# Making the modulation tiles of the last two sub-layers earlier, in steps of half a tile

## The chip, the cores and the metric

The kernel runs on one core of one Trainium2 chip. The metric is the device time of one launch in microseconds (us). A core has TensorE (PE) for matrix products, VectorE (DVE), ScalarE (ACT), GpSimd (POOL) and SyncE (SP). SP issues most loads here.

## The reference

One inference step of a two-layer encoder, for a prompt of 512 frames and a sample of 64 frames (576 columns in all, 1024 channels, float32). Each layer has three sub-layers: a feed-forward, a token mixer and a feed-forward. The mixer of the first layer is a gated delta rule beside a short convolution, that of the second is stick-breaking attention with 16 heads. What matters for this change is the modulation, which each sub-layer takes from a conditioning vector `c` of the prompt and of the sample:

```python
cond = jax.nn.silu(c)
for l in range(DEPTH):
    mod = (cond @ ada_w[l] + ada_b[l]).reshape(b, N_SUB, 3, D_MODEL)
    shift, scale, gate = mod[:, :, 0], mod[:, :, 1], mod[:, :, 2]
    hh = _modulated_norm(x, norm_g[l, 0], shift[:, 0], scale[:, 0])
    x = x + 0.5 * gate[:, 0, None] * _swiglu(hh, ff_w_in[l, 0], ff_w_out[l, 0])
    ...
```

`ada_w[l]` is 1024 x 9216, so that each layer has nine vectors `j` of 1024 channels: shift, scale and gate of sub-layer 0 (`j` 0 to 2), of the mixer (3 to 5) and of the second feed-forward (6 to 8).

## The kernel before, in words

**The order of the work.** The program runs feed-forward (0, 0), mixer 0, feed-forwards (0, 2) and (1, 0), mixer 1 and feed-forward (1, 2). The text calls the feed-forwards the first to the fourth, the fourth also the last. All products are split: a weight and an activation are each written as a high and a low part (`wh`, `wl`; `XH`, `XL`), and three matmuls stand for one. Weights come by SP's DMA into a ring of three `stage` buffers (`w_dma`), ACT copies the high part, and DVE (sometimes POOL with a DMA) makes the low part.

**A feed-forward** (`ffn`, L843) has three chunks of 8, 8 and 6 column tiles of the hidden layer. For each tile it makes gate and up products from `XH` and `XL`, and `HH`, `HL` from them; after each chunk comes an output projection, whose evacuation (`residual`, L752) multiplies by the gate and adds to `x`. The first tiles of the first chunk are plain; the others go through `dense7` (L529), which makes a pair of products in seven block products instead of eight. Its operands are sums of activations (`TH`, `TL`) and of weights (`ss`), made on DVE, and DVE and ACT put the seven results together (`sg`, `up`, `hm`). Behind the last output projection of a sub-layer, the norm for the next one starts (`last_pairs`, L809; `start_sub`, L832).

**Mixer 1** (`mixer1`, L1503) makes q, k and v for eight pairs of heads, and runs one attention task (`att_pair`) for each pair behind the other. For each of nine query blocks, PE makes scores, ACT two sigmoids (`sg`, `sn`), DVE a scan (`cp`) and a product, PE transposes, ACT and DVE copy the result (`wt`), and PE multiplies by v. The tasks run between the dense matmuls of q, k, v, and of the first part of the output projection.

**The planner.** The instructions of each engine run in the order in which the program is written, and that order is made by a scheduler in the kernel (`Sched`, L257) over an account of the engines' times (`Model`). After each group of three dense matmuls, `tick` (L284) lets each task that is due take a step. A task yields the time at which it is next due, on PE's account (`S.clock`); `until` (L296) runs tasks until something has been made. `M.t["DVE"]` is the account of DVE.

**The modulation.** The vectors are made on DVE: a tile of 128 channels of one `j` is a load of 128 x 1024 float32 from `in_ada` into `aw` (`ada_dma`, L762), and for prompt and sample (`g`) one `scalar_tensor_tensor` that multiplies it by the broadcast `cond` (`cb`) and sums along the row into `mod`; the products themselves go to `jk` and are not used (`ada_tile`, L768). The text calls one such instruction a step. `ada_end` adds the bias after eight tiles. `ada_task` (L792) does this for a list of (l, j), a tile per interval `every` (in ns of the account), and only when the account has DVE no more than 1000 ns ahead. With two `aw` buffers (`bufs=2`) the next tile's load is issued just before this tile's steps. With one (`bufs=1`), load and steps of the same tile are apart by part of the interval. `hold` keeps the task back from a sub-layer's last output projections until the next sub-layer's second half has been normed.

Where it is made before: the shifts and scales of feed-forward 0 at the start, (0, 2) to (0, 7) in feed-forward (0, 0) with 6.2 us (L1793), (0, 8) and (1, 0) to (1, 4) in (0, 2) and (1, 0) with 9.5 us (L1802), (1, 5) to (1, 7) in mixer 1 with one buffer and 8.5 us (L1809), and (1, 8) in feed-forward (1, 2) with 8 us (L1814). The norms wait for their shift and scale (`out.need`), `residual` for the gate, and `mixer1` waits for its task before the last part of the output projection (L1668).

Of the kernel before, what the change touches and what calls it, by code (L numbers as in the profile page):

```python
# [107 lines left out]
def outs(nk):  # L108

    n = 2 if nk > 4 else (4 if nk > 2 else 8)  # L110
    return [tuple(range(m, m + n)) for m in range(0, 8, n)]
# [192 lines left out]
def encoder_step(ctx: ExitStack, tc: tile.TileContext, a, o):  # L304
    nc = tc.nc
    M = Model()
# [12 lines left out]
    S = Sched(M, lambda: psum.free("a"))  # L319
# [22 lines left out]
    cb = base.tile([P, 2, D], F32, name="cb")  # L342
# [403 lines left out]
    def split(src, ks):  # L746
        for t0, t1 in HALF:
            for i in ks:
                A.activation(XH[:, i, t0:t1], src[:, i, t0:t1], AF.Copy)
                V.tensor_sub(XL[:, i, t0:t1], src[:, i, t0:t1], XH[:, i, t0:t1].bitcast(F32))  # L750
# [9 lines left out]
    aw = {}  # L760

    def ada_dma(pool, todo, bufs):  # L762
        if todo:
            l, n = todo.pop(0)
            aw[l, n] = pool.tile([P, D], F32, name="aw", bufs=bufs)
            dma(aw[l, n], a["ada"][l, n])

    def ada_tile(pool, cb, l, j, kt):  # L768
        w = aw.pop((l, j * 8 + kt))
        for g in range(2):  # L770
            jk = pool.tile([P, D], mybir.dt.float8e4, name="jk")
            V.scalar_tensor_tensor(jk, w, 1.0, cb[:, g, :], op0=OP.mult, op1=OP.mult,
                                   accum_out=mod[:, l, j, kt, g:g + 1], saturate=False)
# [3 lines left out]
    def ada_end(l, j, k0=0, n=8):  # L777
        if k0 + n == 8:
            made.add((l, j))
        m = mod[:, l, j, k0:k0 + n]  # L780
        b = sm["ada_b"][:, l, j * 8 + k0:j * 8 + k0 + n].unsqueeze(2).to_broadcast([P, n, 2])
        V.tensor_add(m, m, b)
        s, kind = divmod(j, 3)
        if kind == 1:
            gn = sm["norm_g"][:, l * 3 + s, k0:k0 + n].unsqueeze(2).to_broadcast([P, n, 2])
            V.scalar_tensor_tensor(m, m, 1.0, gn, op0=OP.add, op1=OP.mult)
        if kind == 2 and s != 1:
            V.tensor_scalar(m, m, 0.5, None, op0=OP.mult)
# [3 lines left out]
    def ada_task(pool, todo, every, bufs=2):  # L792
        ahead = [(l, j * 8 + kt) for l, j in todo for kt in range(8)]
        for _ in range(bufs - 1):
            ada_dma(pool, ahead, bufs)
        yield S.clock + every
        for l, j in todo:
            for kt in range(8):
                while hold[0]:
                    yield S.clock + 1000.0  # L800
                ada_dma(pool, ahead, bufs)
                if bufs == 1:
                    yield S.clock + every - 3000.0
                ada_tile(pool, cb, l, j, kt)
                yield max(S.clock + (3000.0 if bufs == 1 else every), M.t["DVE"] - 1000.0)
            ada_end(l, j)


# [691 lines left out]
        return last_pairs(npool, 0, 1, ABO[1], modulated(npool, 0, 2))  # L1500


    def mixer1(pool, task, npool, at):  # L1503
        so = pool.tile([P, 8, NT], F32, name="so")
        qbH = pool.tile([P, 9, P], F32R, name="qbH")
        qbL = pool.tile([P, 9, P], F32R, name="qbL")
# [154 lines left out]
        for gi, ks in enumerate(SBO):  # L1661
            S.finish(att_tasks[ks[-1]])
            split(so, ks)
            if gi < len(SBO) - 1:
                for ms in outs(len(ks)):
                    dense(lambda g, half, ps: residual(1, 1, ms[g], half, ps), ks=ks, inter=ms[0] == 0)
            else:
                S.finish(at)  # L1668
                return last_pairs(npool, 1, 1, ks, modulated(npool, 1, 2))


    npool = Ring(M, ctx.enter_context(tc.tile_pool(name="npool", bufs=1)), 1)
# [14 lines left out]
    task = {}  # L1687

    with tc.tile_pool(name="ada", bufs=1) as ap, tc.tile_pool(name="ffn", bufs=1) as fp:
        ap, fp = Ring(M, ap), Ring(M, fp)  # L1690
# [40 lines left out]
        for m in range(8):  # L1731
            for half in range(2):
                stats(npool, m, half, V)
            if m % 2:
                g, h = m // 4, m // 2 % 2
# [55 lines left out]
        feed.scales = scales, scales_out, scales_end  # L1791
        task = feed
        at = S.spawn(ada_task(ap, [(0, j) for j in range(2, 8)], 6200.0))  # L1793
        S2M[0] = True
        task = ffn(0, 0, fp, task, modulated(npool, 0, 1))
        assert at[2]
    with tc.tile_pool(name="m0", bufs=1) as mp:
        mp = Ring(M, mp)
        task = mixer0(mp, task, npool)
    with tc.tile_pool(name="ada", bufs=1) as ap, tc.tile_pool(name="ffn", bufs=1) as fp:  # L1800
        ap, fp = Ring(M, ap), Ring(M, fp)
        at = S.spawn(ada_task(ap, [(0, 8)] + [(1, j) for j in range(5)], 9500.0))  # L1802
        task = ffn(0, 2, fp, task, modulated(npool, 1, 0))
        task = ffn(1, 0, fp, task, modulated(npool, 1, 1))
        assert at[2]
    S2M[0] = False
    with tc.tile_pool(name="m1", bufs=1) as mp:
        mp = Ring(M, mp)
        at = S.spawn(ada_task(mp, [(1, j) for j in (5, 6, 7)], 8500.0, 1))  # L1809
        task = mixer1(mp, task, npool, at)  # L1810
    with tc.tile_pool(name="ffn", bufs=1) as fp:
        fp = Ring(M, fp)
        yo["pool"] = fp
        at = S.spawn(ada_task(fp, [(1, 8)], 8000.0))  # L1814
        task = ffn(1, 2, fp, task, final)
        S.finish(task[0])
        S.finish(task[1])
# [96 lines left out]
```

## Time and profile before

| | |
|---|---|
| time, median of 3 runs | 2474.02 us (2473.24 to 2474.09) |
| the profiled execution | 2477.48 us |
| its span, first to last instruction | 2475.6 us |
| mean granted TensorE clock | 0.969 |
| PE busy, weight loads busy | 2358.8 us, 2278.5 us |
| DVE, ACT, POOL busy | 1784.2, 1091.2, 339.6 us |
| HBM read, written | 261.44 MB, 11.51 MB |

The profile is one execution. Times count from its first instruction. "Busy" of PE is modelled, since matmuls are pipelined: the records of one engine overlap, and a busy time is the length of their union. "Idle before" an instruction, and what ended it, are worked out from the semaphores. In a row, `jk<-aw,cb` means an instruction that writes `jk` from `aw` and `cb`. The helper that issues most instructions is line 191, so nearly all rows have L191, and are told apart by their tiles.

### The profile page before, as it was taken

The page shows a single profiled execution, that of the slowest core. Times are in us where ns is not written, and L with a number is a line of the kernel's source. Part 1 is how long each engine was busy: PE and PEld are TensorE (multiplying, and loading weights), DVE is VectorE, ACT ScalarE, POOL GpSimd, SP SyncE. Part 2 cuts the span into 40 slices and gives each one's busy share as a digit, 9 for nine tenths or more (in the row PEclk, how much of TensorE's full clock was granted, in tenths as well). Part 3 has the DMA queues.
Part 4 walks back from the last instruction along what each step waited for, and adds up shares of the span by engine and source line. Part 5 has one row for each costly group of instructions (what it writes and reads, how often), then busy time and mean ns, then how long its engine had stood idle before and what let it go on. Part 6 is the DMA issues. An engine that isn't in the chain of part 4 may idle for free. (4 is left out here: it accounts for less than half of the span.)

```text
span 2475.6 us, 45399 instructions
## 1 busy us (share of the span) xinstructions
PE 2358.8 (95%) x18364; PEld 2278.5 (92%) x18364; DVE 1784.2 (72%) x3456; ACT 1091.2 (44%) x1984; POOL 339.6 (14%) x467
## 2 busy tenths in 40 slices
PE   7989899999999999999999999999999999999998
PEld 5989899988878899999999999999888879999998
DVE  7688978588687578697967756466567777848474
ACT  4334526443322255263534446255555555425252
POOL 4100000342222240000022000003000004000001
PEclk9999999998889899999999999999999999999999
DMA  6656655232122246465636445352544325322222
GB/s 238 181 170 189 199 180 152 92 103 59 47 67 79 74 125 182 150 207 166 177 119 171 144 111 137 93 130 83 174 138 148 119 81 145 126 87 86 94 90 77
DMA packets 107349, 320.98 MB, mean 130 GB/s; under 512 B 26194, under 2 KB 28498, under 8 KB 106884
## 3 DMA queue, kind: packets, MB, share of 16 engines
q1 hardware_dynamic: 95188, 272.99, 33.0%
q0 software_dynamic: 11952, 45.09, 9.9%
q8 instruction: 145, 2.38, 0.4%
q14 instruction: 64, 0.52, 0.1%
HBM read 261.44 MB, written 11.51 MB: 110 GB/s over the span
## 5 line engine op out<-in xcount | busy, mean ns | idle before, releaser
L191 PE MATMUL d<-XH,wh 128*128 128x288 f32 x2304 | 714.8, 310 | 14.3 <-ACT XH L191 6.1
L191 PE MATMUL d<-XL,wh 128*128 128x288 f32 x2304 | 697.0, 303 | 11.3 <-POOL XL L191 8.0
L191 PE MATMUL d<-XH,wl 128*128 128x288 f32 x2304 | 695.3, 302 | 3.3 <-DMA wl<-stage 1.7
L191 PEld LDWEIGHTS d<-XH,wh 128*128 128x128 f32 x2304 | 447.3, 194 | 27.4 <-ACT XH L191 11.3
L191 PEld LDWEIGHTS d<-XL,wh 128*128 128x128 f32 x2304 | 447.5, 194 | 17.1 <-POOL XL L191 12.4
L191 PEld LDWEIGHTS d<-XH,wl 128*128 128x128 f32 x2304 | 447.2, 194 | 4.9 <-DVE wl L191 2.7
L191 PE MATMUL d<-HH,wh 128*128 128x288 f32 x1408 | 417.9, 297 | 3.9 <-ACT HH L191 3.9
L191 PE MATMUL d<-HL,wh 128*128 128x288 f32 x1408 | 418.3, 297 | 3.5 <-DVE HL L191 3.5
L191 ACT ACTIVATE wh<-stage 128x1024 fp32r<-128x1024 f32 (+3 forms) x345 | 319.9, 939 | 227.9 <-PE d L191 222.5
L191 PE MATMUL d<-HH,wl 128*128 128x288 f32 x1408 | 415.7, 295 | 0.0
L191 DVE TENSOR_TENSOR wl<-stage,wh 128x1024 fp32r<-128x1024 f32 (+3 forms) x259 | 268.7, 1043 | 113.0 <-ACT wh L191 110.6
L191 DVE SCALAR_TENSOR_TENSOR jk<-aw,cb 128x1024 fp8e4<-128x1024 f32 x256 | 315.4, 1232 | 36.0 <-DMA aw<-in_ada 31.4
L191 PE MATMUL d<-TH,wh 128*128 128x288 f32 x1056 | 312.1, 296 | 12.8 <-ACT sg L191 12.7
L191 PE MATMUL d<-TL,wh 128*128 128x288 f32 x1056 | 312.2, 296 | 0.0
L191 PE MATMUL d<-TH,wl 128*128 128x288 f32 x1056 | 311.9, 295 | 0.2
L191 DVE SCALAR_TENSOR_TENSOR x<-d,mod,x 128x64 f32<-128x64 f32 (+2 forms) x384 | 146.6, 412 | 218.3 <-PE d L191 216.8
L191 PEld LDWEIGHTS d<-HL,wh 128*128 128x128 f32 x1408 | 265.7, 189 | 6.2 <-DVE HL L191 6.2
L191 PEld LDWEIGHTS d<-HH,wh 128*128 128x128 f32 x1408 | 265.5, 189 | 4.7 <-ACT HH L191 4.4
L191 PEld LDWEIGHTS d<-HH,wl 128*128 128x128 f32 x1408 | 265.9, 189 | 0.0
L191 PEld LDWEIGHTS d<-TH,wh 128*128 128x128 f32 x1056 | 198.6, 188 | 16.4 <-ACT sg L191 16.3
L191 PEld LDWEIGHTS d<-TH,wl 128*128 128x128 f32 x1056 | 198.8, 188 | 0.8 <-DVE wl L191 0.6
L191 PEld LDWEIGHTS d<-TL,wh 128*128 128x128 f32 x1056 | 198.3, 188 | 0.0
(328 smaller groups left out, 3440.8 us busy)
## 6 DMA issues: line engine op xcount, KB each, us to landing
stage<-in_w SPq DMA_DIRECT2D x301, 512.0 KB
aw<-in_ada SPq DMA_DIRECT2D x128, 512.0 KB
wl<-stage POOLq DMA_DIRECT2D x59, 512.0 KB, 4.6
stage<-in_w SPq DMA_DIRECT2D x36, 384.0 KB
TL<-XL POOLq DMA_DIRECT2D x8, 576.0 KB, 8.6
TL<-ss POOLq DMA_DIRECT2D x8, 576.0 KB, 5.8
TL<-in_ada SPq DMA_DIRECT2D x8, 512.0 KB
stage<-in_w SPq DMA_DIRECT2D x8, 320.0 KB
```

The source lines that it names most:

```text
L191: r = real(*args, **kw)
```

## The change

The task now goes through a tile in two steps, each followed by its own wait; the branch for one buffer goes. The two feed-forwards between the mixers get all of (0, 8) and (1, 0) to (1, 8) with an interval of 8.0 us; mixer 1 and the last feed-forward have no task any more, and mixer 1 doesn't wait for one. The task of the first feed-forward keeps its list and its 6.2 us, but runs through the same loop.

```diff
--- before.py
+++ after.py
@@ -765,9 +765,9 @@
             aw[l, n] = pool.tile([P, D], F32, name="aw", bufs=bufs)
             dma(aw[l, n], a["ada"][l, n])
 
-    def ada_tile(pool, cb, l, j, kt):
-        w = aw.pop((l, j * 8 + kt))
-        for g in range(2):
+    def ada_tile(pool, cb, l, j, kt, gs=(0, 1)):
+        w = aw[l, j * 8 + kt]
+        for g in gs:
             jk = pool.tile([P, D], mybir.dt.float8e4, name="jk")
             V.scalar_tensor_tensor(jk, w, 1.0, cb[:, g, :], op0=OP.mult, op1=OP.mult,
                                    accum_out=mod[:, l, j, kt, g:g + 1], saturate=False)
@@ -799,10 +799,9 @@
                 while hold[0]:
                     yield S.clock + 1000.0
                 ada_dma(pool, ahead, bufs)
-                if bufs == 1:
-                    yield S.clock + every - 3000.0
-                ada_tile(pool, cb, l, j, kt)
-                yield max(S.clock + (3000.0 if bufs == 1 else every), M.t["DVE"] - 1000.0)
+                for g in range(2):
+                    ada_tile(pool, cb, l, j, kt, (g,))
+                    yield max(S.clock + every / 2, M.t["DVE"] - 1000.0)
             ada_end(l, j)
 
 
@@ -1500,7 +1499,7 @@
         return last_pairs(npool, 0, 1, ABO[1], modulated(npool, 0, 2))
 
 
-    def mixer1(pool, task, npool, at):
+    def mixer1(pool, task, npool):
         so = pool.tile([P, 8, NT], F32, name="so")
         qbH = pool.tile([P, 9, P], F32R, name="qbH")
         qbL = pool.tile([P, 9, P], F32R, name="qbL")
@@ -1665,7 +1664,6 @@
                 for ms in outs(len(ks)):
                     dense(lambda g, half, ps: residual(1, 1, ms[g], half, ps), ks=ks, inter=ms[0] == 0)
             else:
-                S.finish(at)
                 return last_pairs(npool, 1, 1, ks, modulated(npool, 1, 2))
 
 
@@ -1799,19 +1797,17 @@
         task = mixer0(mp, task, npool)
     with tc.tile_pool(name="ada", bufs=1) as ap, tc.tile_pool(name="ffn", bufs=1) as fp:
         ap, fp = Ring(M, ap), Ring(M, fp)
-        at = S.spawn(ada_task(ap, [(0, 8)] + [(1, j) for j in range(5)], 9500.0))
+        at = S.spawn(ada_task(ap, [(0, 8)] + [(1, j) for j in range(9)], 8000.0))
         task = ffn(0, 2, fp, task, modulated(npool, 1, 0))
         task = ffn(1, 0, fp, task, modulated(npool, 1, 1))
         assert at[2]
     S2M[0] = False
     with tc.tile_pool(name="m1", bufs=1) as mp:
         mp = Ring(M, mp)
-        at = S.spawn(ada_task(mp, [(1, j) for j in (5, 6, 7)], 8500.0, 1))
-        task = mixer1(mp, task, npool, at)
+        task = mixer1(mp, task, npool)
     with tc.tile_pool(name="ffn", bufs=1) as fp:
         fp = Ring(M, fp)
         yo["pool"] = fp
-        at = S.spawn(ada_task(fp, [(1, 8)], 8000.0))
         task = ffn(1, 2, fp, task, final)
         S.finish(task[0])
         S.finish(task[1])
```

## Rows read from the trace of the kernel before

**Rows 1.** The page's busy times: us (share of the span), instructions of each engine.

```profile
PE 2358.8 (95%) x18364; PEld 2278.5 (92%) x18364; DVE 1784.2 (72%) x3456; ACT 1091.2 (44%) x1984; POOL 339.6 (14%) x467
```

**Rows 2.** Busy time by stretch (us:us length; engines; clock, DMA, GB/s): feed-forwards one to three.

```profile
211.50:309.70 98.20, 91.58 (x674) 89.72 (x673) 95.21 (x162) 55.99 (x93) 6.06 (x7) 1.00 0.66 199
309.70:364.80 55.10, 53.02 (x387) 52.58 (x387) 43.79 (x77) 10.35 (x11) 0.87 (x1) 0.97 0.55 182
1041.00:1131.00 90.00, 89.65 (x674) 89.19 (x673) 83.43 (x140) 56.40 (x93) 6.09 (x7) 1.00 0.65 188
1182.40:1249.20 66.80, 66.80 (x506) 66.80 (x505) 60.54 (x102) 41.45 (x69) 4.33 (x5) 1.00 0.62 177
1249.20:1293.80 44.60, 41.94 (x308) 41.49 (x307) 26.99 (x55) 15.41 (x28) 10.81 (x13) 0.96 0.32 114
1451.70:1540.80 89.10, 89.10 (x674) 89.10 (x674) 63.11 (x100) 56.24 (x93) 6.06 (x7) 1.00 0.53 136
1592.20:1659.00 66.80, 66.80 (x506) 66.80 (x505) 46.74 (x75) 41.21 (x69) 4.30 (x5) 1.00 0.52 130
1659.00:1699.80 40.80, 40.41 (x309) 40.10 (x308) 19.35 (x42) 15.43 (x28) 10.44 (x13) 1.00 0.27 86
```

**Rows 3.** The same stretches, instructions of `jk` alone: length, DVE busy (records).

```profile
211.50:309.70 98.20, 36.21 (x61) 1.00 0.66 199
...
1041.00:1131.00 90.00, 22.20 (x38) 1.00 0.65 188
1182.40:1249.20 66.80, 15.70 (x27) 1.00 0.62 177
```

**Rows 4.** PE's waits, 211 to 310 us: total us, times, longest.

```profile
PE d L191 <- ACT sg L191: 6.6, 8, 1.6
```

**Rows 5.** DVE in order of time, end of the second feed-forward's third chunk.

```profile
1248.33 1.22 DVE L191 SCALAR_TENSOR_TENSOR jk<-aw,cb 128x1024 fp8e4<-128x1024 f32 x1
...
1249.59 1.23 DVE L191 SCALAR_TENSOR_TENSOR jk<-aw,cb 128x1024 fp8e4<-128x1024 f32 x1
...
1250.74 0.45 DVE L191 TENSOR_TENSOR up<-up 128x288 f32<-128x288 f32 x1
```

**Rows 6.** PE's waits, 1249 to 1294 us: total us, times, longest.

```profile
PE d L191 <- ACT HH L191: 2.3, 1, 2.3
```

**Rows 7.** Tile `aw`: steps (ns least/median/most, first, last start); DVE's waits for loads.

```profile
L191 DVE SCALAR_TENSOR_TENSOR jk<-aw,cb x256: 1206/1224/1708, 85.5 to 2140.7; 128x1024 fp8e4<-128x1024 f32 x128
...
  DMA aw<-in_ada: 31.4, 11
```

**Rows 8.** DVE in order of time, first attention pair of mixer 1.

```profile
1747.58 0.23 DVE L191 TENSOR_TENSOR sg<-sg,cp 128x64 f32<-128x64 f32 x1
1756.64 1.22 DVE L191 SCALAR_TENSOR_TENSOR jk<-aw,cb 128x1024 fp8e4<-128x1024 f32 x1 [8.83 <-DMA aw<-in_ada]
...
1759.07 0.42 DVE L191 TENSOR_TENSOR_SCAN cp<-sn,ones 128x128 f32<-128x128 f32 x1
```

**Rows 9.** ACT in order of time, the sigmoid that this scan reads.

```profile
1750.00 0.28 ACT L191 ACTIVATE sn<-a 128x128 f32<-128x128 f32 x1
```

**Rows 10.** Busy time by stretch, mixer 1: attention pairs 0 to 6, and pair 7.

```profile
1730.20:2003.80 273.60, 253.40 (x1943) 232.07 (x1942) 191.99 (x400) 147.87 (x340) 13.39 (x42) 0.98 0.47 140
2003.80:2033.40 29.60, 25.68 (x185) 21.33 (x183) 19.92 (x47) 15.58 (x38) 0.00 (x0) 0.88 0.20 61
```

**Rows 11.** The chain of waits, 1730 to 2004 us, shares of the stretch by line.

```profile
by line: PE d L191 40.9%; PE a L191 23.9%; issue 8.5%; DVE cp L191 7.0%; DVE jk L191 3.6%; DVE sg L191 3.3%; ACT sn L191 2.2%; ACT sg L191 2.1%; DMA wl<-stage 1.7%; ACT wt L191 1.6%; DMA aw<-in_ada 1.5%; DVE x L191 1.3%; DVE wl L191 1.1%; D
```

**Rows 12.** PE's waits at the start of the last feed-forward, 2050 to 2150 us.

```profile
PE d L191 <- ACT sg L191: 3.2, 2, 2.3
```

**Rows 13.** DVE in order of time, start of the third feed-forward.

```profile
1317.46 1.58 DVE L191 SCALAR_TENSOR_TENSOR jk<-aw,cb 128x1024 fp8e4<-128x1024 f32 x1
```

**Rows 14.** POOL in order of time, the same place.

```profile
1317.15 4.27 POOL L191 TENSOR_TENSOR XL<-hf,XH 128x288 fp32r<-128x288 f32 x3 [1.98 <-ACT XH L191]
```

**Rows 15.** Tile `jk`, 880 to 1715 us: steps (ns), first and last start.

```profile
L191 DVE SCALAR_TENSOR_TENSOR jk<-aw,cb x96: 1211/1224/1701, 906.2 to 1393.6; 128x1024 fp8e4<-128x1024 f32 x96
```

## The prediction, made before the changed kernel was run

> **What bounds the kernel now.** I read the page's busy times first: TensorE (PE) is busy 95% of the span, so only what leaves it waiting can be gained [rows 1]. Then I cut the feed-forwards into stretches that hold the same matmuls and compared their lengths [rows 2]. The reader should see equal PE counts with unequal lengths. The middle chunk of a feed-forward (674 PE instructions, eight seven-product pairs) takes 89.1 us in the third feed-forward, which makes no modulation tile there, 90.0 in the second with a tile about every 9.5 us, and 98.2 in the first with one about every 6.7 us. Its VectorE (DVE) is busy 63.11 of 89.1, 83.43 of 90.0 and 95.21 of 98.2 us. So DVE is the second bound: at 93% it costs PE next to nothing, at 97% 9 us. The output projection behind the middle chunk shows it too: 55.1 us in the first feed-forward, against 51.4 for the same work elsewhere (1131.0 to 1182.4, between two stretches of the group). After the third chunk, 44.6 us stand against 40.8.
>
> The modulation steps (`jk`) fill 36.21, 22.20 and 15.70 us of three of these stretches [rows 3]. In the first feed-forward PE waits eight times, 6.6 us in all, for an ACT copy or silu of `sg` [rows 4]; I take these to be late because ACT stands behind a late DVE. One case is seen whole: two steps run back to back from 1248.33 to 1250.74, and `up` and `sg`, the last seven-product evacuations, start the moment they end [rows 5]. PE waits 2.3 us there for `HH` [rows 6].
>
> In the second mixer a tile has one buffer, so its load is issued late, and DVE waits for it at the head of its queue. Of the 31.4 us that DVE waits on tile loads in all [rows 7], 8.83 come at 1756.64, with the scan `cp` of 128 columns right behind the two steps [rows 8], though the `sn` it reads was written from 1750.00 on [rows 9]. Between the start of the first and of the last attention pair (273.6 us) PE is idle 273.6 - 253.4 = 20.2 us [rows 10].
>
> **The change part by part.** Nothing is computed less: the 256 steps of 1224 ns and their 128 tile loads remain [rows 7]. 24 tiles (48 steps, 58.8 us of DVE) leave the second mixer, 8 (16 steps, 19.6 us) leave the last feed-forward, and 64 steps (78.3 us) go into the two feed-forwards between the mixers. Every feed-forward task, the first one's too, now places one step and then yields for half the interval, where it placed two. The planner's rule that no step is placed while its own account has DVE over 1 us ahead now applies before each step, so the account of DVE behind a placed step is at most about 1.0 + 1.2 us, where it was 1.0 + 2.4.
>
> *Second mixer.* On the chain of waits `jk` is 3.6% and its loads 1.5% of the 274 us from 1730 to 2004: 9.9 + 4.1 = 14.0 us [rows 11]. If each engine's order stayed, no more than this could go, since the rest of that chain remains. Below, 0: the next-late thing may be ACT's sigmoids, and with other planned times the order may even get worse, by some 2 us (one wait of the size in rows 6). I take 9: most of the chain's share, because the steps stand directly before scans, less a third for what comes late next. In the last attention pair, without a step, PE is still idle 29.6 - 25.68 = 3.9 us [rows 10], so waits don't vanish with the steps. The final wait for the task is the planner's alone and gives nothing back: the tiles are made before the last attention pair, and it stands behind that pair.
>
> How much room PE has here depends on how its busy time is read. The rows have matmuls busy 253.4 and weight loads 232.07 of 273.6 us [rows 10]. The Trainium skill (Perfetto Trace Analysis, Identifying the Most-Contended Engine) says that matmul occupancy misleads for TensorE, because matmuls are pipelined, and that weight-load occupancy measures the headroom. By it the room would be 41.5 us, not 20.2; the sum here stays with the chain's 14.0, and the larger room is a rival below.
>
> *Last feed-forward.* At its start PE waits 3.2 us for `sg` [rows 12], while DVE does eight tiles. Bounds 0 and 3.2; I take 2.5.
>
> *First feed-forward.* Only the halving acts. Its excess is 98.2 - 89.1 = 9.1 us in the middle chunk and 55.1 - 51.4 = 3.7 behind it [rows 2], 12.8 together. Between all of it (steps only where DVE is free) and a loss of 2 us (a step more often in the way) I take a gain of 5: the lateness that a pair of steps can add is halved, but DVE still has to do 36 us of them. Steps put off fall into the next stretch, where DVE is busy 43.79 of 55.1 us.
>
> *Feed-forwards between the mixers.* A tile each 8.0 us is 89.1 / 8.0 = 11.1 tiles, 27.3 us, over 63.11 of other work: 90.4 of 89.1 us, just over full. So the planner's rule will stretch the interval somewhat. Cost per middle chunk: from 0 to 9.1 us (the first feed-forward's excess); I take 1.5, nearer to the 0.9 that 93% cost, as the lateness is halved. That makes (1.5 - 0.9) + 1.5 = 2.1. The second's third chunk (60.54 of 66.8 busy, no loss yet) I put at 0.5, the two first chunks at 0.5 each. At the chunk's end, one step in the way instead of two gives back about 2 of the 44.6 - 40.8 = 3.8 us, and two more loaded chunk ends cost 0.5 each. Sum: 2.1 + 0.5 + 1.0 - 2.0 + 1.0 = 2.6 us lost, with ends of a gain of 3 and a loss of 25 (the slow rival).
>
> *Loads.* 32 tile loads move into SP's queue between weight loads. With them the third feed-forward's middle chunk would move 136 GB/s plus 512 KiB each 8 us (some 65), 201 in all; the first did 199 [rows 2], and PE's only waits there were for `sg` [rows 4]. I cost them at 0. A tile load waits in SP's queue until the steps of the tile two before have read its buffer, and weight loads queue behind it; three weight buffers cover this, and if they don't, DVE's `ss` and ACT's `wh` wait first.
>
> *POOL.* A step that runs beside POOL's `XL` takes 1.58 us [rows 13], not 1.22, and three `XL` take 4.27 [rows 14]. The Trainium skill (SBUF, section on SBUF's two separate sides) has DVE operations with two SBUF inputs and GpSimd operations that read SBUF lock each other out for a whole instruction. The rows agree that both get longer; by the rule alone all 64 moved steps could pay. By the rows POOL is busy 6.06 of 89.1 us [rows 2], so 64 x 0.07 x 0.36 = 1.6 us of DVE, inside the 2.6.
>
> Sum: 9 + 2.5 + 5 - 2.6 = 13.9 us. The profiled execution took 2477.48 us (span 2475.6), 3.5 over the median of 2474.02; taken from the median, 2460.
>
> **The rivals.** (a) *DVE overfills in the two feed-forwards* (slower). The middle chunks become the first feed-forward's: 8.2 and 9.1 us more; two chunk ends cost 3.7 each; halving gives nothing anywhere. 24.7 lost, 11.5 won in the mixer and the last feed-forward: 2474 + 13.2 = 2487. For it: 90.4 of 89.1. Against: the planner stretches instead of overfilling, with 80 us to spare (48 tiles took from 906 to 1395 [rows 15], 489 us, 33 over 48 x 9.5; 80 x 8 + 33 from 906 ends at 1579, and the third chunk ends at 1659.0 [rows 2]). It decides where those chunks reach 97% of DVE and PE's wait for `sg` reaches 6 us in each. Chance 0.11.
> (b) *The mixer's steps were covered.* ACT and PE latencies take their place and the mixer gives 1: 2474 - 1 - 2.5 - 5 + 2.6 = 2468. For it: PE is 93% busy there. Chance 0.17.
> (c) *The mixer gains more.* With no tile in its account the planner brings attention forward, and fewer pairs run with little other work, like the last one at a granted clock of 0.88 [rows 10]. I price it at 25, between 20.2 and 41.5: 2474 - 25 - 7.5 + 2.6 = 2444. Chance 0.13.
> (d) *It doesn't do what it says*: tiles late, so that gates wait. The eighth tile completes the gate of the second feed-forward, near 906 + 64 = 970; it is wanted at 1041.0 - 51.4 = 989.6. Chance 0.02, about no change.
>
> **How the numbers follow.** The forecast, 2460, has 0.57 and by its bounds a range of its own from 2451 to 2468. Measurement can tell about 0.2%, 5 us. Below 2469 lie nearly all of the forecast (0.55), (c) 0.13 and half of (b), 0.06: 0.74 faster. The other half of (b), (d) and a rest of the forecast make 0.15 the same, (a) 0.11 slower. The range for 8 in 10 goes from 2446 to 2475: it leaves out (a) and the lower half of (c).
>
> **What would show it.** Right: no `jk` after the third feed-forward; the first to the last attention pair some 9 us shorter than 273.6; 674 instructions in about 94 us in the first feed-forward and about 90.5 in the next two; steps singly, some 4 us apart. Wrong: middle chunks of 95 us and more between the mixers (a), pairs as long as before with PE waits ended by ACT (b), or a mixer shorter by over 20 us (c).

## The result, and the profile after

The changed kernel took 2439.82 us (median of 4 runs, 2438.69 to 2440.88), the kernel before 2474.06 on the same chip: a ratio of 0.9865, with an interval from 0.9853 to 0.9877. It is faster by 34 us where 14 were forecast, and lies below the range. The profiled execution took 2440.72 us, with a span of 2438.9 and a granted clock of 0.978 (0.969 before). The page's busy times of the kernel after, beside [rows 1]:

```profile
PE 2340.2 (96%) x18364; PEld 2260.8 (93%) x18364; DVE 1769.1 (73%) x3456; ACT 1090.3 (45%) x1984; POOL 336.6 (14%) x467
```

The counts are the same on every engine, so the same work is done. The next table cuts both spans into sub-layers, from the first dense matmul of one to that of the next, read off the two traces. A feed-forward is cut further: `c1` to `c3` are its chunks, `H1` to `H3` the output projections behind them.

| us | before | after | difference | forecast |
|---|---|---|---|---|
| first feed-forward | 445.26 | 430.19 | -15.1 | -5 |
| its c1, H1, c2 | 132.05, 51.39, 98.28 | 119.41, 52.64, 95.30 | -12.6, +1.3, -3.0 | 0, 0, about -4 |
| its H2, c3 | 55.00, 67.89 | 53.01, 69.18 | -2.0, +1.3 | about -1, 0 |
| mixer 0 | 411.46 | 412.24 | +0.8 | 0 |
| second feed-forward | 409.05 | 408.71 | -0.3 | together |
| third feed-forward | 406.05 | 408.00 | +2.0 | +2.6 |
| mixer 1 | 357.95 | 337.42 | -20.5 | -9 |
| last feed-forward | 406.02 | 401.69 | -4.3 | -2.5 |

How far a single profile can be trusted is seen in the runs below that share a stage. The first feed-forward took 428.85 to 433.96 us in seven profiles with the half steps of the kernel after, and 442.16 to 445.26 in three with the whole steps of the kernel before. Mixer 1 took 337.24 to 341.57 us in seven profiles with the matmul order of the kernel after, and mixer 0 took 406.25 to 416.99 in all. So a difference counts from some 5 us on in the first feed-forward and in mixer 1, from about 2 us on in the other feed-forwards, and in mixer 0 not at all.

Busy time by stretch, kernel after: the first feed-forward's middle chunk and the projection behind it, the second's middle and third chunk and its end, the third's middle chunk, then mixer 1 from the first to the last attention pair and the last pair (columns as in [rows 2] and [rows 10]).

```profile
200.20:295.50 95.30, 91.93 (x674) 89.87 (x673) 92.13 (x156) 55.83 (x93) 6.07 (x7) 1.00 0.70 200
295.50:348.50 53.00, 51.40 (x386) 50.95 (x385) 40.93 (x74) 10.34 (x11) 0.87 (x1) 1.00 0.55 178
1028.50:1118.50 90.00, 89.33 (x674) 89.10 (x673) 84.53 (x144) 56.52 (x93) 6.10 (x7) 1.00 0.67 194
1170.60:1237.80 67.20, 66.93 (x504) 66.70 (x504) 63.05 (x108) 41.43 (x69) 4.34 (x5) 1.00 0.65 184
1237.90:1279.30 41.40, 40.46 (x308) 40.02 (x307) 26.71 (x56) 15.39 (x28) 10.84 (x13) 1.00 0.36 123
1437.50:1527.50 90.00, 89.32 (x674) 89.09 (x673) 84.29 (x142) 56.48 (x93) 6.08 (x7) 1.00 0.68 194
...
1715.90:1966.70 250.80, 239.53 (x1871) 217.60 (x1870) 135.09 (x294) 145.10 (x338) 13.38 (x42) 1.00 0.36 99
1966.70:1997.60 30.90, 29.80 (x237) 27.04 (x237) 23.27 (x54) 16.78 (x41) 0.00 (x0) 1.00 0.30 90
```

The two middle chunks between the mixers take 90.00 us each, although the third feed-forward now has a tile about every 8 us: the half steps fit. The first to the last attention pair take 250.8 us instead of 273.6, and the last pair runs at full clock with 237 matmuls instead of 185, where it ran at 0.88 [rows 10]. The two stretches don't hold the same work: before the last pair there are 1871 matmuls now, and there were 1943. PE's waits of the kernel after, from 200 to 296 us (beside [rows 4]) and, in the second fence, between the attention pairs:

```profile
PE d L191 <- DVE wl L191: 2.3, 4, 0.6
PE d L191 <- ACT sg L191: 0.9, 3, 0.5
```

```profile
PE a L191 <- DVE sg L191: 4.1, 8, 0.8
PE d L191 <- ACT XH L191: 1.8, 1, 1.8
PE a L191 <- ACT sn L191: 1.6, 7, 0.2
```

The eight waits for `sg` in the middle chunk of the first feed-forward, 6.6 us before, have shrunk to 0.9. Tile `aw` of the kernel after: the steps, and VectorE's waits for tile loads (beside [rows 7]):

```profile
L191 DVE SCALAR_TENSOR_TENSOR jk<-aw,cb x256: 1208/1217/1575, 86.1 to 1618.3; 128x1024 fp8e4<-128x1024 f32 x128
...
  DMA aw<-in_ada: 15.0, 11
```

All 256 steps are there, the last at 1618.3, in the third feed-forward. VectorE's waits for loads fell from 31.4 to 15.0 us. By stage they were 15.7 us in the first feed-forward, 0 in the two middle ones, 13.3 in mixer 1 and 2.4 in the last feed-forward; now they are 3.7 in the first feed-forward and 11.3 in the two middle ones.

**The place that the prediction passed over.** 12.6 us of the gain lie in the first chunk of the first feed-forward, where nothing was costed. Busy time by stretch in the kernel before shows where they were lost, from 120 to 138 us:

```profile
120.00:126.00 6.00, 6.00 (x47) 6.00 (x47) 2.61 (x4) 2.63 (x4) 0.00 (x0) 1.00 0.90 257
126.00:132.00 6.00, 2.08 (x14) 1.81 (x12) 5.00 (x7) 1.98 (x4) 0.00 (x0) 0.94 0.09 38
132.00:138.00 6.00, 5.59 (x24) 5.28 (x23) 5.46 (x9) 2.01 (x3) 0.00 (x0) 0.50 0.70 257
```

TensorE does 47 matmuls in the first 6 us, then 14, then 24 at half the granted clock. In order of time, the kernel before on four engines there (start, duration, engine; in brackets how long the engine was idle before, and what ended it). SP's queue:

```profile
114.78 0.33 SPq L327 DMA_DIRECT2D stage<-in_w  x1
115.16 0.42 SPq L327 DMA_DIRECT2D aw<-in_ada  x1
```

VectorE:

```profile
124.58 1.23 DVE L191 SCALAR_TENSOR_TENSOR jk<-aw,cb 128x1024 fp8e4<-128x1024 f32 x1 [3.10 <-DMA aw<-in_ada]
...
125.85 1.23 DVE L191 SCALAR_TENSOR_TENSOR jk<-aw,cb 128x1024 fp8e4<-128x1024 f32 x1
...
129.54 0.45 DVE L191 TENSOR_TENSOR hm<-sg,d 128x288 f32<-128x288 f32 x1
```

ScalarE:

```profile
130.02 0.44 ACT L191 ACTIVATE HH<-hm 128x288 fp32r<-128x288 f32 x1 [7.39 <-DVE hm L191]
130.37 1.04 ACT L191 ACTIVATE wh<-stage 128x1024 fp32r<-128x1024 f32 x1
```

TensorE:

```profile
131.47 0.61 PE L191 MATMUL d<-XH,wh 128*128 128x288 f32 x1 [3.92 <-ACT wh L191]
```

VectorE was ready for the step at 124.58 - 3.10 = 121.48, 6.3 us after SP had issued its load at 115.16, directly behind a weight load. The load landed 124.58 - 115.16 = 9.4 us after its issue; the DMA engines were 0.90 busy around it. The two other waits of this chunk are alike: the steps were due 5.3 and 5.1 us after the issue, and the loads took 9.2 and 8.3. The two steps stood at the head of its queue. Behind them came two sums `TL` of 1.35 us each and `hm`, behind `hm` ACT's `HH`, behind `HH` the weights `wh`, and behind `wh` PE. The 3.92 us of the wait are little more than half of what was lost: between 126 and 138 us, 38 matmuls ran where two stretches like the first hold 94, so 56 are missing, 56 x 6.00 / 47 = 7.1 us.

By the same count the first of the three waits cost TensorE nothing, and the second about 1.4 us (67 matmuls from 110 to 120 us, where 78 fit). Some 4.2 us more were lost at the end of the chunk, where no step waits for a load, but six steps stand within 14 us:

```profile
144.00:150.00 6.00, 5.47 (x42) 5.24 (x41) 5.39 (x12) 0.74 (x2) 0.00 (x0) 1.00 0.45 160
150.00:160.00 10.00, 8.35 (x50) 7.97 (x50) 8.67 (x13) 4.81 (x8) 0.00 (x0) 0.83 0.50 159
```

Between 80 and 147.5 us the kernel after has no such place: its PE is busy without a gap, at a clock of 1.00.

### The profile page after: what moved, and what is told of

Read it like the earlier page. It is cut to its first block, busy times and chain, and to the rows that moved or that the text cites. A ratio compares the mean times of both kernels' runs of the same rounds, so it can differ in the third digit from the quotient of the medians.

```text
span 2438.9 us, 45494 instructions
## 1 busy us (share of the span) xinstructions
PE 2340.2 (96%) x18364; PEld 2260.8 (93%) x18364; DVE 1769.1 (73%) x3456; ACT 1090.3 (45%) x1984; POOL 336.6 (14%) x467
## 4 chain that ended last, share of the span: by engine, by line
PE 68%; DVE 18%; ACT 6%; issue 5%; DMA 2%; POOL 0%; SPq 0%; DVEq 0%; ACTq 0%; POOLq 0%
PE d L191 57%; PE a L191 11%; DVE jk L191 3%; DVE wl L191 2%; DVE iz L191 2%; ACT wh L191 2%; DVE ss L191 1%; DVE hf L191 1%; DMA wl<-stage 1%; DMA aw<-in_ada 1%; DVE t2k L191 1%; DVE hm L191 1%; DVE sg L191 1%; DVE HL L191 1%; ACT sg L191 1%
## 5 line engine op out<-in xcount | busy, mean ns | idle before, releaser
L191 DVE SCALAR_TENSOR_TENSOR jk<-aw,cb 128x1024 fp8e4<-128x1024 f32 x256 | 312.2, 1219 | 15.1 <-DMA aw<-in_ada 15.0
```

The lines of the kernel that those rows point to most:

```text
L191: r = real(*args, **kw)
```

## The experiments

Each was timed against the kernel before on the same chip; a ratio is to that kernel, with its interval in brackets. A diff is against the kernel named in its first sentence. The stage lengths are read off the trace of one profiled execution of each run, as in the table above. The expectations of e1 and e2 count the first feed-forward from the start of the span, 28 us before its first dense matmul.

**Whole steps (e1).** The changed kernel, with both steps of a tile together:

```diff
-                for g in range(2):
-                    ada_tile(pool, cb, l, j, kt, (g,))
-                    yield max(S.clock + every / 2, M.t["DVE"] - 1000.0)
+                ada_tile(pool, cb, l, j, kt)
+                yield max(S.clock + every, M.t["DVE"] - 1000.0)
```

> The changed kernel, but each tile's two steps are placed together again, every 8.0 us (6.2 us in the first feed-forward). Theory: the halving gave the 15 us that the first feed-forward lost in length (473 to 458 us), and it is what keeps the middle feed-forwards cheap; so this kernel has the first feed-forward of before (473 us), the middle ones 5 to 20 us longer than the changed kernel's 817, the mixer as in the changed kernel (337 us): 2460 to 2475 us. Rival, that the first feed-forward got shorter for another reason (a different place of the tiles' loads): it stays at 458 and the time at 2440 to 2445 us.

Measured: 2470.15 us, ratio 0.9988 with an interval from 0.9972 to 1.0004, so no gain that can be told. First feed-forward 444.35, the two between the mixers 418.46 and 417.24, mixer 1 341.57. Moving the tiles alone wins nothing: the middle feed-forwards lose 418.46 + 417.24 - 409.05 - 406.05 = 20.6 us, about what the mixer and the last feed-forward win. That is rival (a), for whole steps. Busy time by stretch of this run, the projection behind the second feed-forward's first chunk and the third's middle chunk, then its PE waits from 870 to 1700 us:

```profile
990.30:1045.70 55.40, 53.03 (x386) 52.59 (x385) 36.92 (x66) 10.33 (x11) 0.88 (x1) 0.97 0.48 154
1466.10:1557.40 91.30, 90.13 (x673) 89.21 (x673) 87.85 (x148) 56.54 (x93) 6.06 (x7) 1.00 0.67 196
```

```profile
PE d L191 <- ACT HH L191: 8.4, 5, 2.1
PE d L191 <- ACT sg L191: 4.6, 9, 1.2
```

The price is not mostly in the middle chunk (91.3 against 90.0) but at the chunk ends: 55.4 us for a projection that takes 51.4 undisturbed, with waits of up to 2.1 us for `HH`. The four projections behind the first and second chunks make 13.3 of the 20.6 us.

**Half steps alone (e2).** The kernel before, whose feed-forwards place half a tile at a time; the tiles stay where they were, and in the mixer they stay whole.

```diff
...
+                for g in range(2):
+                    ada_tile(pool, cb, l, j, kt, (g,))
+                    yield max(S.clock + every / 2, M.t["DVE"] - 1000.0)
```

> The kernel before, with half steps in the feed-forwards alone; lists and intervals stay, and the second mixer keeps its whole tiles and one buffer. Theory: first feed-forward 458 us instead of 473, the chunk end near 1251 us 3 us shorter, the start of the last feed-forward 2 us shorter, the mixer unchanged at 358 us: 2453 to 2459 us. Rival, that halving does nothing alone: 2470 to 2475 us.

Measured: 2453.89 us, 0.9916 (0.9885 to 0.9947). First feed-forward 429.40, its first chunk 119.08; second feed-forward 406.21; last 403.86; mixer 1 360.24. The halving alone makes all of the first feed-forward's gain, and nothing in the mixer, whose TensorE order here is that of the kernel before.

**The planner's account kept as it was (e3, e9).** The changed kernel, with a task in mixer 1 that charges the planner's accounts and issues nothing. e3 charges the 24 loads and the 48 steps, e9 the steps alone.

```diff
...
+        for kt in range(24):
...
+            start = M.issue("SP", [w], [], 60.0)
+            M.t["DMA"] = max(M.t["DMA"], start + 1300.0) + 4.0 * P * D / 300.0
+            M.mark([w], [], M.t["DMA"] + 700.0, "SP")
+            yield S.clock + every - 3000.0
+            for g in range(2):
+                M.issue("DVE", [jk, sc[:, g:g + 1]], [w, cb], D * 1.04 + 240.0)
...
+        S.spawn(ghost_task(mp, 8500.0))
```

In e9 the three lines of the load are left out.

> The changed kernel, but in the second mixer a task charges the planner's accounts for the old steps and loads without issuing any, so that the program has the order of before there and the steps are gone. Theory of the order (the mixer gained because the planner, rid of the steps, placed attention and dense work otherwise): the mixer keeps most of its old length, 348 to 356 us, and the kernel takes 2450 to 2458 us. Theory of the time (the steps' own time on DVE and the late loads were the cost): the mixer takes 337 to 341 us, the kernel 2440 to 2444 us.

> As the kernel with the ghost task, but only the 48 steps are charged to the planner's account of DVE in the second mixer, not the 24 loads that they wait for. With steps and loads charged the mixer took 348.5 us, with nothing charged 337.4 and, in two other kernels with the same mixer, 340.6 and 341.6. Theory that the order suffers from the charged waits for loads: 337 to 342 us, the kernel 2439 to 2445 us. Theory that the charged DVE time is enough: 345 to 350 us, the kernel 2447 to 2453 us.

Measured: e3 2453.77 us, 0.9914 (0.9886 to 0.9942); e9 2435.95, 0.9842 (0.9825 to 0.9860). All of mixer 1 by stretch: the kernel before, after, e3 and e9, one fence each.

```profile
1699.90:2057.80 357.90, 329.18 (x2478) 302.05 (x2477) 250.47 (x543) 195.31 (x447) 37.35 (x69) 0.96 0.41 124
```

```profile
1687.30:2024.75 337.45, 320.38 (x2479) 294.42 (x2477) 194.92 (x443) 193.49 (x447) 35.41 (x69) 0.99 0.33 94
```

```profile
1688.70:2037.30 348.60, 325.02 (x2479) 299.07 (x2477) 194.29 (x443) 195.00 (x447) 35.56 (x69) 0.98 0.32 91
```

```profile
1693.00:2024.60 331.60, 316.96 (x2478) 293.49 (x2477) 194.38 (x443) 193.73 (x446) 35.38 (x69) 1.00 0.34 96
```

What the orders are can be counted in the traces. The mixer has 940 matmuls that aren't dense, the attention's and some others, and each stands behind a number of dense ones. In e3 these numbers are those of the kernel before, to within 3. In the kernel after, the 940 stand 82 dense matmuls earlier in the mean, up to 171: the planner has brought attention forward, and more dense work is left beside the last pair.

So e3 has the old order, with steps and loads really gone, and its mixer takes 348.6 us: 9.4 less for steps and loads together. The other 11.1 of the 20.5 us come from the order that the planner makes once its account is free. With the spread of the mixer between profiles (337.24 to 341.57 with the new order, 357.95 and, in e2, 360.24 with the old one) the two shares are good to some 4 us. Of what was charged, the loads spoiled the order here: with the steps charged and the loads not (e9), the planner makes a third order, 51 dense matmuls earlier than before in the mean, and the mixer is shorter still. That is one run of each; that charged loads spoil the order in general isn't shown.

**The tiles made twice (e4, e6).** The changed kernel; mixer 1 makes 24 tiles once more into a scratch that nothing reads, and the planner's accounts don't see it, so the order of the other work stays. e6 does the 48 steps from one tile that is loaded once.

```diff
...
+            w = pool.tile([P, D], F32, name="gw")
+            nc.sync.dma_start(w, a["ada"][1, 40 + kt])
+            yield S.clock + every - 3000.0
+            for g in range(2):
+                jk = pool.tile([P, D], mybir.dt.float8e4, name="gj")
+                nc.vector.scalar_tensor_tensor(jk, w, 1.0, cb[:, g, :], op0=OP.mult, op1=OP.mult,
+                                               accum_out=sc[:, g:g + 1], saturate=False)
...
+        S.spawn(dummy_task(mp, 8500.0))
```

> The changed kernel, but the second mixer loads 24 tiles and runs their 48 steps once more, into a scratch tile and unknown to the planner, so that PE's order is that of the changed kernel and the steps are back. Theory of the order: 2440 to 2446 us, the mixer at 338 to 343 us. Theory of the time: the mixer at 350 to 358 us, the kernel at 2452 to 2460 us.

> The changed kernel with the 48 unplanned steps once more in the second mixer, all from one tile that is loaded once, so that no load goes late through SP's queue. With the loads that mixer took 387 us, without steps 337. Theory of the loads (SP's queue was blocked, and DVE stood waiting): 340 to 352 us, the kernel 2443 to 2455 us. Theory of the steps (each stands before scans that PE's order wants at once): 365 to 387 us, the kernel 2467 to 2487 us.

Measured: e4 2487.16 us, 1.0055 (1.0034 to 1.0077), mixer 387.47; e6 2460.65, 0.9953 (0.9929 to 0.9977), mixer 357.39. Steps that the planner doesn't know cost 357.39 - 337.42 = 20.0 us, and the loads another 30.1. Both are far more than the planned steps and loads cost in e3 (9.4), and neither run fell into one theory's numbers. TensorE's order in both is exactly that of the changed kernel. PE's waits in mixer 1 of e4, SP's, and VectorE's:

```profile
PE a L191 <- DVE sg L191: 26.8, 16, 6.5
PE a L191 <- DVE cp L191: 14.2, 4, 7.7
```

```profile
SPq L815 <- DVE cp L191: 29.6, 9, 9.1
SPq L815 <- DMA gw<-in_ada: 23.6, 8, 4.0
```

```profile
DVE gj L819 <- DMA gw<-in_ada: 21.8, 6, 6.3
```

The load (line 815 there) waits in SP's queue for its buffer, all weight loads behind it; VectorE waits 21.8 us for the tile with scan and product behind it, and PE waits for those two, 41.0 us.

**Two buffers in the mixer (e5).** The kernel before, where the mixer's task loads one tile ahead as the feed-forwards do.

```diff
-        at = S.spawn(ada_task(mp, [(1, j) for j in (5, 6, 7)], 8500.0, 1))
+        at = S.spawn(ada_task(mp, [(1, j) for j in (5, 6, 7)], 8500.0))
```

> The kernel before, with two tile buffers in the second mixer, so that each tile is loaded one tile ahead and its two steps are placed together every 8.5 us. Theory that the late loads were the mixer's cost: DVE's 13 us of waits for loads there go, the mixer takes 344 to 350 us instead of 358, the kernel 2460 to 2467 us. Theory that the steps' DVE time and the order were: 354 to 359 us, the kernel 2470 to 2476 us.

Measured: 2469.56 us, 0.9983 (0.9968 to 0.9998), mixer 357.47. The mixer is as long as before, but it isn't the same mixer: with other planned times the planner made another order (the 940 matmuls stand up to 75 dense ones away from where they were). Nor does the second buffer bring the loads in time: VectorE's waits for tiles there fall only from 13.3 to 9.8 us. So a second buffer alone wins nothing, and what loads in time would win in the mixer this run doesn't show.

**Early loads, whole steps (e12).** e1, with each tile's load issued 2 us of the account behind the steps that free its buffer, instead of just before the next tile's steps.

```diff
-        for _ in range(bufs - 1):
+        for _ in range(bufs):
             ada_dma(pool, ahead, bufs)
...
-                ada_dma(pool, ahead, bufs)
                 ada_tile(pool, cb, l, j, kt)
-                yield max(S.clock + every, M.t["DVE"] - 1000.0)
+                yield S.clock + 2000.0
+                ada_dma(pool, ahead, bufs)
+                yield max(S.clock + every - 2000.0, M.t["DVE"] - 1000.0)
```

> The run with whole steps (e1), and each tile's load issued about 4 us of the account earlier, 2 us behind the steps that free its buffer. Nothing else is changed; both steps of a tile still stand together. In e1 VectorE waits 9.9 us for tile loads in the first feed-forward's first chunk, in the changed kernel 2.6, and that chunk takes 131.1 and 119.4 us. Theory of the step's length: the chunk is long because two steps stand together in front of what TensorE waits for. Then the waits for loads fall to some 3 us or less, and the chunk stays at 129 to 132, the first feed-forward at 440 to 445, the run near 2470. Rival, the late load: the waits are the larger part of the 11.7 us. Then the chunk falls to 121 to 125, the first feed-forward to 433 to 438, the run to some 2462. The two middle feed-forwards, where whole steps cost 19 us and VectorE waits little for loads, tell nothing here; both theories leave them at 833 to 838 together.

Measured: 2462.82 us, 0.9956 (0.9939 to 0.9972). First feed-forward 438.50, just above the rival's numbers; its first chunk 118.80, even below them; the two middle ones 413.45 + 418.81 = 832.3. The first chunk by stretch in the kernel before, after, and e12:

```profile
28.00:160.00 132.00, 116.96 (x822) 111.80 (x823) 102.18 (x160) 52.54 (x101) 33.34 (x25) 0.94 0.54 162
```

```profile
28.00:147.50 119.50, 110.81 (x822) 107.68 (x823) 96.35 (x151) 53.50 (x101) 33.34 (x25) 0.97 0.56 168
```

```profile
28.40:147.20 118.80, 111.23 (x824) 107.64 (x825) 97.31 (x152) 53.37 (x100) 33.19 (x25) 0.97 0.58 172
```

VectorE's waits for tile loads in the first feed-forward's first chunk (28 to 148 us), in the kernel before and in the one after:

```profile
DVE jk L191 <- DMA aw<-in_ada: 10.3, 3, 3.9
```

```profile
DVE jk L191 <- DMA aw<-in_ada: 2.6, 2, 1.4
```

In e12 there is none. Whole steps with loads in time win the first chunk's 12.6 us as well, so the length of a step alone doesn't cost them. But e12 also places fewer steps in this chunk: 19, against 22 in the kernel before and in e1, and 18 in the kernel after. Here e5 helps, whose first feed-forward has the order and the 22 steps of the kernel before. By chance its loads came otherwise: the step behind the load at 115 us found it landed. TensorE's stretch where the kernel before did 14 matmuls, and VectorE's waits for tile loads in this chunk (28 to 156 us), in e5:

```profile
126.00:132.00 6.00, 5.31 (x40) 5.07 (x40) 4.97 (x9) 2.74 (x4) 0.00 (x0) 1.00 0.26 73
```

```profile
DVE jk L191 <- DMA aw<-in_ada: 6.7, 2, 6.0
```

The same steps in the same order took 132.05 us with 10.3 us of waits, 131.12 with 9.9 (e1) and 127.06 with 6.7 (e5). So the late loads are shown as the cause of the larger part. The loss at the end of the chunk is there in e5 too (5.2 us from 138 to 155 us), with no late load beside it; those 4 to 5 us may come of the late loads before, or of the steps that crowd there, and no run took that apart.

Behind that chunk whole steps still cost: the rest of the first feed-forward is 438.50 - 118.80 = 319.7 us against 430.19 - 119.41 = 310.8 with halves, and the middle feed-forwards 832.3 against 816.7. So half steps are worth 8.9 and 15.6 us there, against whole steps with early loads; against whole steps with late ones (e1: 313.2 and 835.7) it is 2.4 and 19.0. In e1 the late loads cost 131.12 - 118.80 = 12.3 us in the first chunk, but only 444.35 - 438.50 = 5.9 over the whole feed-forward, since what is won there is partly given back behind it, where the third chunk then has 16 steps instead of 8.

**No step at a chunk's end (e7, repeated as e11), and the changed kernel again (e10).** The task waits while the planner's clock is 5.5 to 15.5 us behind the start of a chunk's last pair.

```diff
...
+                    while quiet[0] <= S.clock < quiet[1]:
+                        yield S.clock + 500.0
...
+                if jj == nj - 1:
+                    quiet[:] = S.clock + 5500.0, S.clock + 15500.0
```

> The changed kernel, but no step is placed from 5.5 us after the start of a chunk's last pair until 15.5 us after it, in every feed-forward. Theory (what halving left over is a step in front of the last evacuations of a chunk): the output projections behind chunks, 52.6, 53.0, 52.6, 52.0, 52.6 and 52.0 us, return to 51.4 to 51.6, 5 us less in all, 2434 to 2436 us. Rival (the steps crowd elsewhere): what is won there is lost in the middle chunks, 2438 to 2442 us.

> The kernel with the quiet chunk ends, beside the changed kernel. By its profile (2429.2 against 2438.9 us, output projections and chunks between them shorter) it is 5 to 10 us under the changed kernel: ratio to before 0.982 to 0.985. Rival, that the gain was the chip's spread: the same ratio as the changed kernel's within 0.001.

> The changed kernel once more, beside the next one on the same chip: 0.985 to 0.988 of the time before, by the first comparison.

Measured: e7 2434.54 us, 0.9840 (0.9817 to 0.9862); e11 2431.69, 0.9821 (0.9804 to 0.9838); e10, on the chip of e11, 2438.15, 0.9855 (0.9836 to 0.9874). The projection behind the first feed-forward's first chunk, after and in e7:

```profile
147.60:200.20 52.60, 51.37 (x386) 50.92 (x385) 40.53 (x73) 10.35 (x11) 0.88 (x1) 1.00 0.57 184
```

```profile
148.10:199.50 51.40, 51.21 (x387) 50.98 (x386) 38.63 (x70) 10.35 (x11) 0.88 (x1) 1.00 0.56 181
```

The projections go back to 51.4 us, the three feed-forwards win 3.3, 4.0 and 1.7 us in e7. With 2431.69 against 2438.15 this is the fastest version that was run, although the two intervals still touch, and the lead over the changed kernel is not certain.

**Longer intervals (e8).** The changed kernel with 6.9 and 8.6 us between tiles instead of 6.2 and 8.0.

```diff
-        at = S.spawn(ada_task(ap, [(0, j) for j in range(2, 8)], 6200.0))
+        at = S.spawn(ada_task(ap, [(0, j) for j in range(2, 8)], 6900.0))
...
-        at = S.spawn(ada_task(ap, [(0, 8)] + [(1, j) for j in range(9)], 8000.0))
+        at = S.spawn(ada_task(ap, [(0, 8)] + [(1, j) for j in range(9)], 8600.0))
```

> The changed kernel with longer intervals, 6.9 us instead of 6.2 in the first feed-forward and 8.6 instead of 8.0 in the middle ones. Theory (DVE is over full in the first feed-forward's middle chunk, 92.13 of 95.3 us): that chunk falls from 95.3 to 90 to 93 us, the middle feed-forwards stay within 1 us, 2435 to 2438 us. Rival (the planner stretches the intervals by itself already, the rest is where steps fall): 2438 to 2442 us.

Measured: 2441.77 us, 0.9867 (0.9842 to 0.9892), no gain, as the rival has it. The first feed-forward's middle chunk by stretch in this run:

```profile
199.30:290.90 91.60, 90.86 (x674) 89.69 (x673) 88.92 (x152) 55.75 (x93) 6.07 (x7) 1.00 0.70 202
```

The middle chunk falls from 95.3 to 91.6 us, but steps are left over (19 instead of 16 in the third chunk, 5 instead of none in the last projection), and the last projection takes 43.56 us instead of 40.65, and the rest is within what single profiles differ by.

## Why the prediction was wrong, point by point

- **What bounds the kernel**: that TensorE is slowed where VectorE is late held. What failed is the use of the 31.4 us of load waits. That 8.83 of them come in the mixer is right, but the others were given no place, and 10.3 were in the first chunk of the first feed-forward. Its length, 132.0 us, got no cost, because only chunks with equal matmuls were compared.
- **First feed-forward, 5 us, "only the halving acts"**: this is the step that failed first. At the two places where it was costed it was right: 3.0 + 2.0 = 5.0 us. But 12.6 us came in the first chunk, which the sum put at nothing. With half steps VectorE waits 2.6 us there for tile loads instead of 10.3; that these waits were the cause of the larger part, e12 shows by taking them away with whole steps, and e5 by its shorter waits in the same order. 2.5 us were given back in H1 and c3. In c3 there are now 16 steps instead of 8. In H1 there are 17 instead of 18, and e7, which keeps steps away from the end of the chunk, gets its 1.3 us back.
- **Second mixer, 9 us, bounds -2 and 14.0**: the steps and their loads are worth 9.4 us (e3), as forecast. The bound failed in its condition, "if each engine's order stayed": the order changed and gave 11.1 us more. That is the mechanism of rival (c), with 20.5 for its price of 25. Its signs are there too: attention stands 82 dense matmuls earlier, and the last pair's clock went from 0.88 to 1.00. What it put down to tiles in general lies, by e9 against e3, in the loads that the planner had charged.
- **The headroom**: the prediction read it between the first and the last attention pair, 20.2 us without a matmul. 22.8 us went there, but the stretch also holds 72 matmuls fewer now, so the two can't be compared. Over the whole mixer the work is the same. No matmul was busy for 357.90 - 329.18 = 28.7 us before; 20.5 us were won. The same 2478 or 2479 matmuls were busy 329.18 us before and 320.38 after, so 8.8 of the 20.5 us came out of matmul busy time: it also holds slow work, and is no bound. The Trainium skill (Perfetto Trace Analysis, Identifying the Most-Contended Engine) says to judge TensorE's headroom by its FLOP rate and by weight-load busy time, not by matmul busy time. The trace agrees so far, but can't say which is the better measure: weight loads leave 357.90 - 302.05 = 55.9 us, the gain lies within both, and their busy time fell too, to 294.42.
- **Last feed-forward, 2.5 us, bounds 0 and 3.2**: 4.3. The 3.2 us of waits for `sg` [rows 12] are gone; 1.1 us more than the bound went with them. By e2, which keeps the eight tiles there and halves their steps, 2.2 of the 4.3 us come from the halving alone; where the 1.1 us lie is open.
- **Feed-forwards between the mixers, -2.6 us**: a loss of 408.71 + 408.00 - 815.10 = 1.6 us, and of 1.0 in the second profile (407.85 + 408.20). The middle chunks were forecast at about 90.5 and took 90.0, the second's end gave back 44.57 - 41.39 = 3.2 us for 2 forecast, and the four projections behind first and second chunks cost 0.6 to 1.2 us each, 3.5 together, for 1.0 forecast. The term was right in its sum, and only because of the half steps: whole ones cost 20.6 (e1), and 17.2 with early loads (e12).
- **Loads, 0**: right in its sum for the 32 that moved: the middle feed-forwards lost 1.6 us in all, although VectorE now waits 11.3 us there for tile loads, where it waited for none. Wrong as a view of loads: the waits of those that stayed in the first feed-forward changed, and there 10.3 us of waits went with 12.6 us of TensorE's time.
- **POOL, 1.6 us of VectorE**: that both get longer, the prediction's rows show for the step alone; the trace shows it for `XL` too, with a median of 0.81 us with no step beside it and 1.77 with one. But the moved steps did not all get longer: the median step is 1217 ns and the longest 1575, and of the 160 steps in the two middle feed-forwards two took more than 1.3 us. That all 64 would pay isn't seen.
- **The rivals**: (a) holds for whole steps, at 20.6 us for 24.7 forecast, but through the chunk ends more than the middle chunks; half steps keep it away. (b) fell: the steps' time came out almost whole. (c) gave the mixer; its 2444 is the nearest number, partly because the first feed-forward's surplus stands in for the mixer's 4.5 missing ones. (d) did not occur. In the chances, "half of (b), 0.06" is a third of its 0.17.

Left open: why mixer 0, which the change doesn't touch, varies from 406 to 417 us between profiles; why half steps alone give the loads more time (in the kernel after, the steps of the first chunk's second to seventh tile are due 5.5 to 8.6 us after the issue of their load; before, by turns, some 5 to 6 and 9 to 11 us); what the last 4 us of the first chunk's gain come from; what loads in time would give in the mixer; and what early loads, half steps and quiet chunk ends give together, which wasn't run.

## What to carry to other kernels

Small filler work on an in-order engine is paid at the place where it stands, not by its sum: with 256 steps in the same stages, the kernel took 2470 us with pairs of steps (e1), 2463 with pairs and early loads (e12), and 2440 with single steps. A wait is paid in the same way: 10.3 us of VectorE's waits for loads went with 12.6 us of TensorE's time in one chunk, and 11.3 us of such waits with a net loss of 1.6 in two other feed-forwards. Before costing such a step, list every wait for its load by stage, and follow what stands behind it on its engine to the engine that bounds. Where a planner orders the work, taking an item out of its account is a change of its own; test it by charging the account without the work, and the work without the account.

## What the hardware showed that was not expected

- One wait of 3.92 us at TensorE was followed by 6 us with a granted clock of 0.50, that is 1.2 of 2.4 GHz: 24 matmuls where 47 ran before. The wait and the slow stretch together lost 7.1 us.
- Matmul busy time of the same instructions fell by 8.8 us in mixer 1, and by 116.96 - 110.81 = 6.2 us in the first chunk of the first feed-forward, as the granted clock rose from 0.96 to 0.99 and from 0.94 to 0.97.
- A load of 512 KiB issued with 5 to 6 us to spare was late: it took 8.3 to 9.4 us where the DMA engines were 0.8 to 0.9 busy (three loads in the first chunk of the kernel before).
- In mixer 1, 24 loads outside the plan cost more (30.1 us) than the 48 steps on VectorE that they feed (20.0 us), by one profile of e4 and one of e6.
